# A two-block transformer kernel: the 16 extra tokens of the by-token projections computed feature-major and transposed, and v of the second block in 512-wide products

## The chip, the cores and the metric

The kernel runs on one core of a Trainium2 chip. The metric is device time in microseconds (us), the median of several executions. The engines are TensorE (PE, with its weight loads shown as a lane of its own, PEld), VectorE (DVE), ScalarE (ACT), GpSimd (POOL) and the queue that issues most transfers (SP).

## The reference

The input is x of 512 tokens by 1024 features; 16 learned extra tokens are put ahead of them, T = 528 tokens in all. What matters here:

```
# first block
xn   = rmsnorm(concat(meta_tokens, x), ln1_w)
proj = xn @ w_in            # dq, dk, dv, gq, gk, gv, gr, zf, zb
# dv (512 wide): values of a softmax attention over all 528 tokens, 4 heads
# gv (512 wide): values of a gated linear attention, 4 heads
h = x + concat(da, go) @ w_out
h = h + peer_ffn(rmsnorm(h, ln2_w))
x = rmsnorm(h, final_norm_w)
# second block
z = rmsnorm(x, mix_norm) @ w_in_2      # z_pool, u, v, two gates; 1024 features each
v = rmsnorm(gelu(v), sgu_norm)         # then mixed over the tokens of each chunk of 128
...                                    # gates, a convolutional feed-forward, a last gate
```

All of it is float32 in and out.

## The kernel before, in words

**Products.** Activations lie feature-major: X is [128 partitions, 8, 528], the feature index split over partitions and KD = 8 slices, the 512 tokens first and the 16 extra tokens (N_META) last. Every operand of a large product is split into a high and a low part in a rounded format, and `mm3` (line 97) adds three matmuls per slice: high by high, high by low, low by high. A matmul has a stationary operand, which a weight load brings into the array, and a moving operand, whose columns stream through. `load_w` fetches a weight tile and `split` makes its two parts, the high one by an ACT copy (line 73), the low one by a DVE subtraction (line 74), each in two halves, with four buffers of each kind. A weight tile of 512 KB therefore gives two high and two low halves of [128, 512 elements].

**Two layouts of a result.** Most projections keep features on the partitions: weights are stationary, tokens move (`product`, `halved`, `linear`). The values dv, gv and v are needed with tokens on the partitions, so there the tokens are stationary and weight columns move. For gv and dv that is `by_token` (lines 296 to 308). It handles 256 weight columns at a time, from two weight tiles of four slices: for each of five token blocks (four of 128, one of the 16 extra tokens) it takes a PSUM bank, runs 24 matmuls, and ACT scales the result by the token's norm factor `rcol` and writes it (line 307). After each token block it yields.

`by_token` is called four times: once directly for the first half of gv, then three times inside the generator `projections` (second half of gv, two halves of dv). `projections` is a list of filler work that other stages draw from: `fill(n)` advances it by n yields, and `until(...)` advances it until a named result exists. The linear attention draws 20 yields in its first half and 16 in its second; then the softmax attention draws one per query tile in heads 0 and 1, a few in heads 2 and 3 (at most four, since AFTER is 4), two after head 3, and the rest at its end. The last items of `projections` are eight output projections `out_proj(4, m)`, each 12 matmuls of 512 columns and one yield. The softmax attention itself goes, for each head and query tile, through `scores` (matmul line 646, maximum, exponential line 653), transposes (line 666) and `values` (line 676).

The order of instructions on each engine is made from the order of the program by a list scheduler that works with its own estimates of durations, so an instruction can be placed ahead of earlier ones of its engine that are not ready by those estimates.

**v of the second block.** `branches` computes v with tokens on the partitions: for each half f2 of the 1024 features it holds four PSUM banks of 512 columns, one for each token block, and fills each bank in two parts of 256 columns from weight tiles of four slices by 256 columns. Between the two parts of the first half `factors` computes the norm statistics, which end in a reduction by PE (line 110), a second one (line 1162), and the per-token factors (line 1327). The Gelu of line 1335 then reads the banks.

Of the kernel before, what the change touches and what calls it, by code (L numbers as in the profile page):

```python
# [8 lines left out]
F32 = mybir.dt.float32  # L9
# [6 lines left out]
ALU = mybir.AluOpType  # L16
# [4 lines left out]
P = 128  # L21
D = 1024
KD = D // P
SEQ = 512
NT = SEQ // P
N_META = 16
T = SEQ + N_META
# [162 lines left out]
def mixer_block(c):  # L190

    nc, tc, I = c.nc, c.tc, c.I
    with ExitStack() as ctx:
        bp = ctx.enter_context(tc.tile_pool(name="b1", bufs=1))
        wk = ctx.enter_context(tc.tile_pool(name="b1k", bufs=2))
# [3 lines left out]
        def bank(name="mm"):  # L199
            return ps.tile([P, 512], F32, tag="mm", name=name)  # L200
# [15 lines left out]
        xh, xl = operands(c, T)  # L216
# [32 lines left out]
        R = bp.tile([P, T], F32, name="rstd1")  # L249
# [13 lines left out]
        for t in range(NT + 1):  # L263
            n = P if t < NT else N_META
            if t % 2 == 0:
                g2 = two(2 * SEQ) if t < NT else bank()[:, None, :]
            o = g2[:, t % 2, :]
# [20 lines left out]
        rcol = bp.tile([P, NT + 1], F32, name="rcol")  # L288
        o = bank("pr")
        for t in range(NT + 1):  # L290
            n = P if t < NT else N_META
# [4 lines left out]
        def by_token(src, res, fs):  # L296

            for f in fs:
                fs = slice(256 * f, 256 * f + 256)
                ws = [src(False) for _ in range(2)]  # L300
                for t in range(NT + 1):
                    n = P if t < NT else N_META
                    tk = slice(t * P, t * P + n)
                    o = bank()[:n, :256]
                    c.mm3([o], [((xh[:, k, tk], xl[:, k, tk]), [(ws[k // 4][0].row(k % 4), ws[k // 4][1].row(k % 4))])
                                for k in range(KD)])
                    nc.scalar.mul(res[:n, t, fs], o, rcol[:n, t:t + 1])
                    yield

        gv = bp.tile([P, NT + 1, 512], F32, name="gv")  # L310
# [176 lines left out]
        for p in range(2):  # L487
# [65 lines left out]
            for l, s in enumerate(LEVELS + (0,)):  # L553
# [22 lines left out]
                for t in range(NT):  # L576
                    tk = slice(t * P, (t + 1) * P)
# [11 lines left out]
            for i, h in enumerate((2 * p, 2 * p + 1)):  # L589
                hs = slice(64 * i, 64 * i + 64)  # L590
                o = bank("go")
                for t in range(NT):
                    tk = slice(t * P, (t + 1) * P)
# [26 lines left out]
        o = bank()  # L620
# [509 lines left out]
def second_block(c):  # L1130
    nc, tc, I, X = c.nc, c.tc, c.I, c.X[:, :, :SEQ]
    with ExitStack() as ctx:
        bp = ctx.enter_context(tc.tile_pool(name="b2", bufs=1))
        wk = ctx.enter_context(tc.tile_pool(name="b2k", bufs=2))
# [13 lines left out]
        n1 = Norm(c, wk, c.fmw)  # L1148
        R = bp.tile([P, SEQ], F32, name="R01")
# [17 lines left out]
            nc.vector.tensor_tensor(R, R, R0, ALU.mult)  # L1167
            return R0, o

        jobs = [(I["w_v"][f, q], (4, 256)) for f in range(4) for q in range(2)]  # L1170
        jobs.insert(4, (I["w_zpool"][0], (KD, P)))
        for g in range(len(WINDOWS)):
            jobs += [(I[name][2 * g + k], (KD, P)) for name in ("w_zpool", "w_u") for k in range(2) if g or k or name == "w_u"]
# [8 lines left out]
        weights = c.weights(jobs)  # L1182
# [6 lines left out]
        with ExitStack() as actx:  # L1189
# [5 lines left out]
            for m in range(KD):  # L1195
                t = []
# [11 lines left out]
            for m in range(KD):  # L1208
                o = linear(of(mh, ml))
# [91 lines left out]
def branches(c, ap, wk, n1, R, factors, s_out, y_out, bank, tmp, weights, linear):  # L1301

    nc, tc, I, X = c.nc, c.tc, c.I, c.X[:, :, :SEQ]
    vn = ap.tile([P, NT, D], F32, tag="mh", name="vn")
    misc = ap.tile([P, 4, D], F32, tag="ml", name="misc")
    junk, gn, bs, ws = (misc[:, i, :] for i in range(4))
    bs, ws = (v.rearrange("p (h t) -> p h t", h=KD) for v in (bs, ws))
    sc = ap.tile([P, 3, NT], F32, name="sc")
    mk = ap.tile([P, P], F32, name="mk")
    inv = ap.tile([P, len(WINDOWS), PAD], F32, name="inv")  # L1310

    for f2 in range(2):
        banks = [bank() for _ in range(NT)]
        for f in range(2):
            for q in range(2):
                wh, wl = next(weights)
                for t in range(NT):
                    tk = slice(t * P, (t + 1) * P)
                    c.mm3([banks[t][:, f * 256:f * 256 + 256]],
                          [((n1.hi[:, 4 * q + k, tk], n1.lo[:, 4 * q + k, tk]), [(wh.row(k), wl.row(k))]) for k in range(4)],  # L1320
                          first=q == 0, last=q == 1)
            if f2 == 0 and f == 0:
                R0, o = factors()
        if f2 == 0:
            z0 = linear(n1.pairs)
            for t in range(NT):
                nc.tensor.matmul(o[:, t:t + 1], R[0:1, t * P:(t + 1) * P], c.ones[0:1, 0:1], start=True, stop=True)
            nc.vector.tensor_copy(sc[:, 0, :], o[:, :NT])
            nc.sync.dma_start(out=gn, in_=I["sgu_norm"].partition_broadcast(P))
            nc.sync.dma_start(out=bs, in_=I["b_spatial"].partition_broadcast(P))  # L1330
            nc.sync.dma_start(out=ws, in_=I["w_spatial"])
            nc.sync.dma_start(out=mk, in_=I["c_causal"])
            nc.sync.dma_start(out=inv, in_=I["c_inv"])
        for t in range(NT):
            nc.scalar.activation(out=vn[:, t, f2 * 512:(f2 + 1) * 512], in_=banks[t], func=AF.Gelu, scale=sc[:, 0, t:t + 1])
    nc.vector.tensor_tensor(ws, ws, mk[:, None, :].to_broadcast([P, KD, P]), ALU.mult)
    for t in range(NT):
        i = nc.scalar.activation(out=junk, in_=vn[:, t, :], func=AF.Square, accum_out=sc[:, 1, t:t + 1])
    with tc.issue_after(i.ins):
        nc.scalar.preload_act_table_set("natural_log_exp_and_others")  # L1340
    nc.scalar.activation(out=sc[:, 2, :], in_=sc[:, 1, :], func=AF.Ln, scale=1.0 / D, bias=c.eps)
    nc.scalar.activation(out=sc[:, 2, :], in_=sc[:, 2, :], func=AF.Exp, scale=-0.5)
    for t in range(NT):
        nc.vector.scalar_tensor_tensor(vn[:, t, :], vn[:, t, :], sc[:, 2, t:t + 1], gn, op0=ALU.mult, op1=ALU.mult)

    def pool(w, g, y, o):

        z = wk.tile([P, PAD + SEQ], F32, tag="z", name="z")
        nc.vector.memset(z[:, :PAD], 0.0)
        nc.vector.tensor_tensor(z[:, PAD:], o, R, ALU.mult)  # L1350
        s, d = z, 1
        while d < w:
            n = wk.tile([P, PAD + SEQ], F32, tag="zs", name="zs")
            nc.vector.memset(n[:, :PAD], 0.0)
            nc.vector.tensor_tensor(n[:, PAD:], s[:, PAD:], s[:, PAD - d:PAD + SEQ - d], ALU.add)
            s, d = n, 2 * d
        nc.vector.scalar_tensor_tensor(y, s[:, PAD:], 1.0 / w, z[:, PAD:], op0=ALU.mult, op1=ALU.subtract)
        nc.vector.tensor_tensor(y[:, :PAD], s[:, PAD:2 * PAD], inv[:, g, :], ALU.mult)
        nc.vector.tensor_tensor(y[:, :PAD], y[:, :PAD], z[:, PAD:2 * PAD], ALU.subtract)

    def gated(h):
        o = linear(n1.pairs)
        u = tmp("g0")
        nc.vector.tensor_tensor(u, o, R, ALU.mult)
        nc.scalar.activation(out=u, in_=u, func=AF.Gelu)
        o = bank()
        for t in range(NT):
            nc.tensor.matmul(o[:, t * P:(t + 1) * P], vn[:, t, h * P:(h + 1) * P], ws[:, h, :], start=True, stop=True)
        m = tmp("g1")
        nc.vector.tensor_tensor(m.rearrange("p (t i) -> p t i", t=NT), o.rearrange("p (t i) -> p t i", t=NT),  # L1370
                                bs[:, h:h + 1, :].to_broadcast([P, NT, P]), ALU.add)
        nc.vector.tensor_tensor(m, m, u, ALU.mult)
        split_plain(c, s_out[0][:, h, :], s_out[1][:, h, :], m)

    for g, w in enumerate(WINDOWS):
        ph = wk.tile([P, 2, SEQ], F32R, tag="ph", name="ph", bufs=1)
        pl = wk.tile([P, 2, SEQ], F32R, tag="pl", name="pl", bufs=1)
        for k in range(2):
            y = tmp("g0")
            pool(w, g, y, linear(n1.pairs) if g or k else z0)  # L1380
            split_plain(c, ph[:, k, :], pl[:, k, :], y)
        for h in (2 * g, 2 * g + 1):
            gated(h)
            nc.vector.scalar_tensor_tensor(X[:, h, :], X[:, h, :], c.final_norm_w[:, h:h + 1], R0, op0=ALU.mult, op1=ALU.mult)
        wh, wl = next(weights)
        for m in range(2):
            o = bank()
            c.mm3([o], [((wh.row(2 * m + k), wl.row(2 * m + k)), [(ph[:, k, :], pl[:, k, :])]) for k in range(2)])
            f = 2 * g + m
            split_scaled(c, y_out[0][:, f, :], y_out[1][:, f, :], o, c.pool_scale_2[:, f:f + 1])  # L1390
# [13 lines left out]
def pack_t(w):  # L1404
    k, m = w.shape
    return np.ascontiguousarray(w.reshape(k // P, P, m // P, P).transpose(2, 1, 0, 3))


def pack_n(w, kc=4, m=256):
    k, n = w.shape  # L1410
    return np.ascontiguousarray(w.reshape(k // (kc * P), kc, P, n // m, m).transpose(3, 0, 2, 1, 4))
# [6 lines left out]
def pack(a):  # L1418
# [23 lines left out]
    I["u_t"] = np.ascontiguousarray(u.reshape(P, NKEYS, KD, P).transpose(1, 3, 2, 0))  # L1442
    I["v_t"] = np.ascontiguousarray(v.reshape(P, NKEYS, 2, 512).transpose(1, 0, 2, 3))
    w = a["w_in_2"][0]
    I["w_zpool"], I["w_u"], I["w_v"] = pack_t(w[:, :D]), pack_t(w[:, D:2 * D]), pack_n(w[:, 2 * D:3 * D])
    I["w_gates"] = np.stack([pack_t(w[:, 3 * D:4 * D]), pack_t(w[:, 4 * D:])])
    I["w_branch"] = np.stack([pack_t(a["w_branch_a_2"][0]), pack_t(a["w_branch_b_2"][0])])
    I["w_out2"] = pack_t(a["w_out_2"][0])
# [56 lines left out]
```

## Time and profile before

| | |
|---|---|
| median of 3 executions | 2463.1 us |
| lowest, highest | 2460.37, 2471.28 us |
| the profiled execution, its own time | 2468.12 us |
| its span, first to last instruction | 2466.4 us |
| mean granted TensorE clock in it | 0.987 of full speed |

The profile and the trace are of one execution; its span and its own time are 1.7 us apart. A busy share counts time with at least one instruction of the engine in flight. Matmuls overlap: one lasts longer than the step from its start to the next one's start. The granted clock is 1.0 at 2.4 GHz and 0.5 at 1.2 GHz.

### The profile page before, as it was taken

What the parts mean: (1) busy time and instruction counts of PE and PEld (TensorE: products, weight loads), DVE (VectorE), ACT (ScalarE), POOL (GpSimd) and SP (SyncE); (2) the same over time, 40 slices, a digit from 0 to 9 for tenths busy, and PEclk for the clock granted to TensorE, in tenths of its full rate; (3) what the DMA queues carried; (4) which work ended last, traced back from release to release, by engine and by line L of the source; (5) the groups of instructions that cost most, each with busy time, mean ns of one, the idle gap of its engine ahead of it and who ended that gap; (6) DMA issues with size and microseconds to landing.
All of it is one profiled execution on the core that took longest, in us unless ns stands there. A gap on an engine that the chain in (4) does not pass through costs nothing.

```text
span 2466.4 us, 34671 instructions
## 1 busy us (share of the span) xinstructions
PE 2402.0 (97%) x12603; PEld 2084.6 (85%) x12603; DVE 1758.2 (71%) x3426; ACT 1194.7 (48%) x2155; POOL 367.3 (15%) x260
## 2 busy tenths in 40 slices
PE   8999899999999999999999998999999999999998
PEld 7887578999999999888778788878888888888888
DVE  5775659999899886886676775866764456777436
ACT  5434553446788995433333333335433335544335
POOL 0000000001333323333242342420000000000000
PEclk9999999999999999999999999999999999999999
DMA  4210033356999999988888889953232232233332
GB/s 138 69 52 26 27 128 137 104 187 202 335 358 348 329 332 361 364 299 295 309 283 289 321 291 311 311 175 106 87 98 94 95 102 96 94 97 98 94 105 103
DMA packets 170297, 471.81 MB, mean 191 GB/s; under 512 B 14060, under 2 KB 66157, under 8 KB 166798
## 3 DMA queue, kind: packets, MB, share of 16 engines
q1 hardware_dynamic: 133262, 335.37, 39.8%
q0 software_dynamic: 36864, 134.23, 15.7%
q8 instruction: 99, 1.62, 0.3%
q14 instruction: 72, 0.59, 0.1%
HBM read 421.31 MB, written 48.23 MB: 190 GB/s over the span
## 4 chain that ended last, share of the span: by engine, by line
PE 62%; DMA 9%; issue 6%; DVE 5%; POOL 2%; ACT 1%; SPq 0%; DVEq 0%; POOLq 0%; ACTq 0%
PE mm L97 49%; PE acc L1105 8%; DMA at<-Ad 3%; DMA row<-in_v_t_dram,ev 3%; PE G L987 3%; POOL row L802 2%; DVE wlo L74 1%; DMA row<-in_peer_u_dram,eu 1%; DMA wraw<-in_v_t_dram 1%; DVE acc L823 1%; PE sc L886 1%; DMA gt<-Gd 1%; DVE row L815 0%; SPq L1064 0%; DVE eq L939 0%
## 5 line engine op out<-in xcount | busy, mean ns | idle before, releaser
L73 ACT CAST whi<-wraw 128x512 fp32r<-128x512 f32 (+3 forms) x902 | 547.4, 609 | 900.8 <-PE mm L97 521.3
L74 DVE TENSOR_TENSOR wlo<-wraw,whi 128x512 fp32r<-128x512 f32 (+3 forms) x902 | 595.4, 670 | 260.6 <-ACT whi L73 256.6
L97 PE MATMUL mm<-hi,whi 128*128 128x384 f32 (+3 forms) x2016 | 721.4, 363 | 16.3 <-ACT fresh L790 9.3
L97 PE MATMUL mm<-lo,whi 128*128 128x384 f32 (+3 forms) x2016 | 717.9, 361 | 0.7 <-DVE lo L182 0.5
L97 PE MATMUL mm<-hi,wlo 128*128 128x384 f32 (+3 forms) x2016 | 717.0, 361 | 0.4 <-DVE wlo L74 0.4
L97 PEld LDWEIGHTS mm<-hi,whi 128*128 128x128 f32 (+1 forms) x2016 | 376.3, 188 | 56.2 <-ACT fresh L790 10.2
L97 PEld LDWEIGHTS mm<-hi,wlo 128*128 128x128 f32 (+1 forms) x2016 | 376.0, 188 | 38.2 <-DVE wlo L74 1.7
L97 PEld LDWEIGHTS mm<-lo,whi 128*128 128x128 f32 (+1 forms) x2016 | 376.1, 188 | 38.1 <-issue 1.7
L1105 PE MATMUL acc<-wlo,wh 128*128 128x512 f32 x768 | 304.0, 396 | 20.9 <-DVE wlo L74 20.7
L802 POOL DMA_INDIRECT row<-in_peer_u_dram,eu x128 | 168.4, 1316 | 930.0 <-DMA wraw<-in_u_t_dram 544.4
L1105 PE MATMUL acc<-whi,wl 128*128 128x512 f32 x768 | 302.2, 394 | 0.0
L802 POOL DMA_INDIRECT row<-in_v_t_dram,ev x128 | 198.7, 1552 | 333.6 <-ACT whi L73 239.2
L1105 PE MATMUL acc<-whi,wh 128*128 128x512 f32 x768 | 248.1, 394 | 0.0
L823 DVE SCALAR_TENSOR_TENSOR acc<-row,act,acc 128x1024 f32<-128x1024 f32 x128 | 163.8, 1280 | 46.0 <-DMA row<-in_v_t_dram,ev 46.0
L1105 PEld LDWEIGHTS acc<-wlo,wh 128*128 128x128 f32 x768 | 146.3, 191 | 56.1 <-DVE wlo L74 25.7
L815 DVE SCALAR_TENSOR_TENSOR row<-row,hn 128x1024 f32<-128x1024 f32 x128 | 155.6, 1218 | 26.6 <-DMA row<-in_peer_u_dram,eu 26.3
L1105 PEld LDWEIGHTS acc<-whi,wh 128*128 128x128 f32 x768 | 146.0, 190 | 30.7
L1105 PEld LDWEIGHTS acc<-whi,wl 128*128 128x128 f32 x768 | 146.3, 190 | 30.3
L984 ACT ACTIVATE oa<-oa,tr 128x128 f32<-128x128 f32 x384 | 122.6, 393 | 21.5 <-DVE oa L982 21.1
L987 PE MATMUL G<-ob,oa 128*128 128x128 f32 x768 | 113.1, 277 | 1.2 <-ACT oa L984 1.2
L987 PEld LDWEIGHTS G<-ob,oa 128*128 128x128 f32 x768 | 108.9, 191 | 2.3 <-ACT oa L984 2.2
L988 ACT COPY gst<-G 128x512 f32<-128x512 f32 x96 | 102.1, 1070 | 16.1 <-PE G L987 15.2
(359 smaller groups left out, 3048.6 us busy)
## 6 DMA issues: line engine op xcount, KB each, us to landing
wraw<-in_u_t_dram SPq DMA_DIRECT2D x128, 512.0 KB, 5.3
wraw<-in_v_t_dram SPq DMA_DIRECT2D x128, 512.0 KB, 7.1
Gd<-gst SPq DMA_DIRECT2D x24, 1024.0 KB, 6.3
gt<-Gd SPq DMA_DIRECT2D x16, 1536.0 KB, 13.0
wraw<-in_w_up_dram SPq DMA_DIRECT2D x44, 512.0 KB, 3.4
Ad<-ast SPq DMA_DIRECT2D x24, 768.0 KB, 5.6
at<-Ad SPq DMA_DIRECT2D x24, 768.0 KB, 12.3
wraw<-in_w_pq_dram SPq DMA_DIRECT2D x16, 512.0 KB, 4.2
```

What stands on the lines that cost most here:

```text
L73: self.step = nc.scalar.copy(hi[i], x)
L74: nc.vector.tensor_tensor(lo[i], x, hi[i].bitcast(F32), ALU.subtract)
L97: nc.tensor.matmul(o, a, b, start=first and ps == 0 and i == 0, stop=last and ps == 2 and i == n - 1)
L802: i = nc.gpsimd.indirect_dma_start(out=t, out_offset=None, in_=table, in_offset=bass.IndirectOffsetOnAxis(ap=idx[:, s:s + 1], axis=0))
L815: nc.vector.scalar_tensor_tensor(u, u, 1.0, hn, op0=ALU.mult, op1=ALU.mult, accum_out=c.act3[:, s:s + 1])
L823: nc.vector.scalar_tensor_tensor(c.acc3, v, c.act3[:, s:s + 1], c.acc3, op0=ALU.mult, op1=ALU.add)
L886: nc.tensor.matmul(o[:, t * P:(t + 1) * P], q[:, t * P:(t + 1) * P], keys[:, f, :], start=True, stop=True)
L984: nc.scalar.mul(oa[:, i, :], oa[:, i, :], tr[:, 2, b0 + i:b0 + i + 1])
L987: nc.tensor.matmul(o[:, i * P:(i + 1) * P], oa[:, i, :], ob[:, i, :], start=True, stop=True)
L988: nc.scalar.copy(st[:, :, b0 - t0:b0 - t0 + TB].rearrange("p j n -> p n j"), o.rearrange("p (n j) -> p n j", n=TB))
L1105: nc.tensor.matmul(acc[2 * t + hf], x[:, jb, tk], y.row(hf), start=n_done == 1 and pi == 0, stop=last2 and bi == len(batch) - 1 and pi == 2)
```

## The change

In `by_token` the 16 extra tokens leave the loop over token blocks. They are computed first, feature-major: for each of the two groups of 128 weight columns, the weights are stationary and the 16 tokens move, into one bank of 32 columns. DVE multiplies this by the norm factors R of those tokens into the tile `me`. After the second token block, PE transposes the two parts of `me` into a bank and ACT copies it to its place. The loop yields four times instead of five.

In `branches`, v's weight tiles become two slices by 512 columns instead of four slices by 256; a tile now fills all 512 columns of the four banks, and four tiles make a half. `factors` stands behind the third of the four tiles.

```diff
             for f in fs:
                 fs = slice(256 * f, 256 * f + 256)
                 ws = [src(False) for _ in range(2)]
-                for t in range(NT + 1):
-                    n = P if t < NT else N_META
-                    tk = slice(t * P, t * P + n)
-                    o = bank()[:n, :256]
+
+                mt = slice(SEQ, T)
+                o = bank()[:, :2 * N_META]
+                for i in range(2):
+                    c.mm3([o[:, i * N_META:(i + 1) * N_META]],
+                          [((ws[k // 4][0].row(k % 4)[:, i * P:(i + 1) * P], ws[k // 4][1].row(k % 4)[:, i * P:(i + 1) * P]),
+                            [(xh[:, k, mt], xl[:, k, mt])]) for k in range(KD)])
+                me = wk.tile([P, 2, N_META], F32, tag="kmt", name="me")
+                nc.vector.tensor_tensor(me, o.rearrange("p (i n) -> p i n", i=2), R[:, None, SEQ:].to_broadcast([P, 2, N_META]), ALU.mult)
+                for t in range(NT):
+                    tk = slice(t * P, (t + 1) * P)
+                    o = bank()[:, :256]
                     c.mm3([o], [((xh[:, k, tk], xl[:, k, tk]), [(ws[k // 4][0].row(k % 4), ws[k // 4][1].row(k % 4))])
                                 for k in range(KD)])
-                    nc.scalar.mul(res[:n, t, fs], o, rcol[:n, t:t + 1])
+                    nc.scalar.mul(res[:, t, fs], o, rcol[:, t:t + 1])
+                    if t == 1:
+                        o = bank()[:N_META, :256]
+                        for i in range(2):
+                            nc.tensor.transpose(o[:, i * P:(i + 1) * P], me[:, i, :], c.ident)
+                        nc.scalar.copy(res[:N_META, NT, fs], o)
                     yield
...
-        jobs = [(I["w_v"][f, q], (4, 256)) for f in range(4) for q in range(2)]
+        jobs = [(I["w_v"][f, q], (2, 512)) for f in range(2) for q in range(4)]
...
     for f2 in range(2):
         banks = [bank() for _ in range(NT)]
-        for f in range(2):
-            for q in range(2):
-                wh, wl = next(weights)
-                for t in range(NT):
-                    tk = slice(t * P, (t + 1) * P)
-                    c.mm3([banks[t][:, f * 256:f * 256 + 256]],
-                          [((n1.hi[:, 4 * q + k, tk], n1.lo[:, 4 * q + k, tk]), [(wh.row(k), wl.row(k))]) for k in range(4)],
-                          first=q == 0, last=q == 1)
-            if f2 == 0 and f == 0:
+        for q in range(4):
+            wh, wl = next(weights)
+            for t in range(NT):
+                tk = slice(t * P, (t + 1) * P)
+                c.mm3([banks[t]],
+                      [((n1.hi[:, 2 * q + k, tk], n1.lo[:, 2 * q + k, tk]), [(wh.row(k), wl.row(k))]) for k in range(2)],
+                      first=q == 0, last=q == 3)
+            if f2 == 0 and q == 2:
                 R0, o = factors()
```

## Rows read from the trace of the kernel before

**Rows 1.** The page: busy shares, and the chain that ended last by engine.

```profile
PE 2402.0 (97%) x12603; PEld 2084.6 (85%) x12603; DVE 1758.2 (71%) x3426; ACT 1194.7 (48%) x2155; POOL 367.3 (15%) x260
...
PE 62%; DMA 9%; issue 6%; DVE 5%; POOL 2%; ACT 1%; SPq 0%; DVEq 0%; POOLq 0%; ACTq 0%
```

**Rows 2.** Windows: length, busy by engine, granted clock, DMA; by_token calls, v stage.

```profile
33.05:51.40 18.35, 18.35 (x127) 15.63 (x126) 3.11 (x7) 8.98 (x19) 0.00 (x0) 0.91 0.01 4
70.50:88.00 17.50, 17.50 (x167) 16.36 (x166) 10.51 (x26) 5.75 (x9) 0.00 (x0) 1.00 0.10 31
177.20:194.00 16.80, 16.80 (x154) 15.62 (x152) 12.76 (x26) 7.10 (x13) 0.00 (x0) 1.00 0.01 1
214.00:240.80 26.80, 25.61 (x173) 19.64 (x171) 15.63 (x36) 12.31 (x31) 0.00 (x0) 1.00 0.01 1
1676.20:1739.70 63.50, 63.50 (x456) 59.55 (x455) 38.24 (x62) 35.30 (x59) 0.00 (x0) 1.00 0.25 82
```

**Rows 3.** Timeline of PE (start, duration in us): a 16-token block, its successor.

```profile
85.20 0.29 PE L97 MATMUL mm<-whi,hi 128*16 128x256 f32 x1
...
87.95 0.40 PE L97 MATMUL mm<-hi,whi 128*128 128x512 f32 x1
```

**Rows 4.** Weight loads grouped by shape: busy us, mean ns, idle before.

```profile
L97 PEld LDWEIGHTS mm<-whi,lo 128*128 128x128 f32 x256 | 49.4, 194 | 0.0
...
L97 PEld LDWEIGHTS mm<-wlo,hi 128*16 128x16 f32 x32 | 3.0, 94 | 0.9 <-issue 0.3
```

**Rows 5.** Timeline of PE: short matmuls with loads of 128 columns.

```profile
52.83 0.39 PE L327 MATMUL mm<-tri,g 16*128 16x16 f32 x2
53.15 0.38 PE L322 MATMUL mm<-tri,g 128*128 128x128 f32 x1
...
1709.58 1.05 PE L1327 MATMUL ps_r<-ones,R 1*128 1x1 f32 x8
```

**Rows 6.** Timeline of PE in the last head of the softmax attention.

```profile
308.46 0.81 PE L646 MATMUL mm<-k,q 64*128 64x264 f32 x1 [2.11 <-ACT pe L653]
...
318.36 0.60 PE L666 MATMUL mm<-ident,pe 128*128 128x128 f32 x4
```

**Rows 7.** Instructions of the tile km: minimum, median, maximum ns.

```profile
L281 DVE TENSOR_TENSOR km<-mm,rstd x2: 152/154/155, 24.8 to 64.4; 128x16 f32<-128x16 f32 x2
```

**Rows 8.** Timeline of PE in the v stage.

```profile
1693.47 1.02 PE L110 MATMUL ps_r<-nacc,ones 128*128 128x512 f32 x2
...
1710.56 0.39 PE L97 MATMUL mm<-whi,hi 128*128 128x256 f32 x1
...
1728.78 0.40 PE L97 MATMUL mm<-hi,whi 128*128 128x512 f32 x1
...
1739.69 0.38 PE L1368 MATMUL mm<-misc,vn 128*128 128x128 f32 x2
```

**Rows 9.** Windows: stretches around falls of the granted clock (column after POOL).

```profile
31.00:34.40 3.40, 3.40 (x23) 2.61 (x24) 0.91 (x3) 0.93 (x2) 0.00 (x0) 1.00 0.53 154
34.40:37.80 3.40, 3.40 (x14) 2.64 (x13) 0.00 (x0) 0.00 (x0) 0.00 (x0) 0.50 0.00 0
37.80:41.20 3.40, 3.40 (x26) 2.89 (x25) 0.00 (x0) 2.78 (x6) 0.00 (x0) 1.00 0.00 0
...
256.20:263.10 6.90, 6.76 (x22) 3.40 (x20) 5.62 (x13) 2.21 (x6) 0.00 (x0) 0.51 0.00 0
...
266.50:269.90 3.40, 3.40 (x5) 1.33 (x4) 2.28 (x7) 0.79 (x2) 0.00 (x0) 0.50 0.00 0
...
307.40:314.30 6.90, 5.84 (x16) 4.29 (x17) 4.71 (x14) 3.21 (x9) 0.00 (x0) 0.51 0.14 40
```

**Rows 10.** Timeline of PE ahead of the first fall.

```profile
31.43 0.59 PE L268 MATMUL mm<-w,zT 33*128 33x512 f32 x1
31.95 1.18 PE L292 MATMUL pr<-ones,rstd 1*128 1x1 f32 x10
```

**Rows 11.** Waits of PE from 230 to 331 us: total us, times, longest.

```profile
PE mm L646 <- ACT pe L653: 8.2, 5, 2.6
```

More of the change, by code (lines that the diff above doesn't have):

```diff
@@ L1444, in pack @@
     w = a["w_in_2"][0]
-    I["w_zpool"], I["w_u"], I["w_v"] = pack_t(w[:, :D]), pack_t(w[:, D:2 * D]), pack_n(w[:, 2 * D:3 * D])
+    I["w_zpool"], I["w_u"], I["w_v"] = pack_t(w[:, :D]), pack_t(w[:, D:2 * D]), pack_n(w[:, 2 * D:3 * D], 2, 512)
     I["w_gates"] = np.stack([pack_t(w[:, 3 * D:4 * D]), pack_t(w[:, 4 * D:])])
```

## The prediction

> **What bounds the kernel now.** I read the page's busy shares and its chain first [rows 1]. TensorE (PE) has a matmul in flight for 97% of the span, and the chain that ended last runs through PE for 62% of it, more than through any other resource. The first question for an edit that touches matmuls is therefore whether PE is full where the edit lies. The windows answer it [rows 2]: in the stretches that hold the four calls of by_token, PE is busy for 18.35 of 18.35, 17.50 of 17.50, 16.80 of 16.80 and 25.61 of 26.80 us, and through the v stage for 63.50 of 63.50. So PE time removed or added there goes to the end nearly one to one, while ScalarE (ACT) and VectorE (DVE) have room. A busy PE hides how fast it goes, since matmuls overlap. What counts is the step from one start to the next, read from the timeline, and the granted clock, read from windows.
>
> **The change part by part: what is removed.** Each call of by_token ends with 24 matmuls whose stationary operand is the 16 tokens and whose moving operand is 256 weight columns. One such block starts at 85.20 and the next matmul behind it at 87.95 [rows 3]: 2.75 us, a step of 0.115. Four calls give 11.0 us. An ACT eviction of a 16-partition tile goes too.
>
> **What is added.** Operands swap: 128 weight columns become stationary and 16 tokens move. That takes 2 x 8 x 3 = 48 matmuls per call, each with its own load of 128 columns. The trace has no such matmul of 128 rows. Its stream of columns is short, so the load decides. A load of 16 columns lasts 94 ns and one of 128 lasts 194 [rows 4]: 100 ns for 112 columns, so about 0.114 us for 128 if each column costs the same. The nearest matmuls agree: eight with a 128-column load and one moving column take 1.05 us in all [rows 5], from which the last one's own time comes off (0.25, an estimate: the 256-column ones beside it last 0.28): 0.80 over seven steps, 0.114. I take 0.115. Below it I set 0.107, a little under both; above it 0.133, from two matmuls of 16 columns with a 128-column load, though of 16 rows: 0.39 us in all, or 0.13 without the last one's own 0.26 (the same estimate), and 0.16 each from 52.83 to the next start at 53.15 [rows 5]. So a call pays 48 x 0.115 = 5.5 us where it paid 2.75.
>
> Two transposes per call come on top. Four of them in a row take 0.60 us [rows 6], so about 0.11 a step, 0.2 us per call. The scaling by R is a DVE operation on 128x32; its neighbour on 128x16 takes 154 ns [rows 7]. The transposes stand behind two whole token blocks, 48 matmuls or 5.8 us after the narrow ones, so DVE has that long before PE waits; without that cover it would cost up to about 1 us per call, the wait for one operation ahead of it in DVE's queue. The new copy by ACT replaces the eviction that went. I count all three at nothing.
>
> By_token alone: 5.5 + 0.2 - 2.75 = +2.95 us per call, **+11.8 us** for four. With 0.107 it is +10.3, with 0.133 it is +15.3.
>
> **The v stage.** 384 matmuls of 256 columns become 192 of 512. From 1710.56 to 1728.78 there are 151 of the narrow kind: 0.1207 a step. From 1728.78 to 1739.69 there are 48 wide ones: 0.2273 [rows 8]. Two narrow less one wide is 0.0141 us, times 192 is **-2.7 us**. Loads (eight of 512 KB) and splits (128x512) keep their sizes. The statistics (factors) now stand behind three of four weight tiles of the first half instead of two. In the trace their first reduction on PE is at 1693.47 [rows 8], about where three tiles end when the stage starts near 1673: 72 x 0.227 = 16.4 plus the slow start. I count the move at nothing. If it is late instead, the Gelu evictions and then the four banks of the second half are, and it costs up to 3 us.
>
> Sum so far: 11.8 - 2.7 = **+9.1 us**.
>
> **The clock.** This is the larger unknown. The windows show the granted clock at half, 1.2 instead of 2.4 GHz, after stretches in which PE did little streaming, and being busy did not save it [rows 9]: from 31.0 to 34.4 PE is busy for all 3.40 us, but until about 33.1 with matmuls of 33 rows or 1 row [rows 10], and from 34.4 to 37.8 the clock is 0.50. Then 14 matmuls start where 26 start in the next equal stretch. The other falls in this block come in the attention, where matmuls have 64 rows and gaps. A new narrow block streams 16 columns in each 0.115 us, a sixteenth of what the block before it streams, for 5.5 us on end. I expect that to look like the first case. Its price from rows: the four low stretches of this block last 3.4, 6.9, 3.4 and 6.9 us, 5.2 on average [rows 9]; at half clock half of that is lost, 2.6 us. Four blocks: **+10.4 us**. The ends are 0 (the clock holds, because the loads count as work) and about 5 us per block, 20 in all, if the narrow block itself runs at 0.23 a step for most of its length and the wide matmuls behind it start low.
>
> **Moved work.** by_token hands control back after each token block, and now does so four times instead of five. Three of its calls feed the fillers of the linear attention and the softmax attention, so everything behind them comes three fillers earlier: three of the four output projections that so far run in the last head's tail move up to the second head. The tail is where PE waits for softmax (8.2 us in five waits over the attention [rows 11], one of 2.11 before 308.46 [rows 6]). A block of output projection is 12 matmuls of about 0.23, 2.8 us, so up to 8.4 us could be uncovered there; against it, the idle time and the low clock in the second head (3.4 us lost of the 6.9 from 256.2) could be filled. Nothing at the middle, 5 us to either side.
>
> One rule of the Trainium skill speaks against the swap itself: TensorEngine Tiling (Array Packing), section When to Use Tiling, says that where the moving dimension is 64 or less one should exchange stationary and streaming operands. The 16 tokens are the stationary operand today; the change does the opposite. The loads of 94 and 194 ns say the same in this kernel, and the sum above is what it costs.
>
> **The rivals.**
> - *Load-bound and the clock falls* (the forecast): 9.1 + 10.4 = +19.5 us. For it: [rows 4, 5, 9]. Against it: no row shows 128-row loads with almost no streaming.
> - *Load-bound, the clock holds*: +9.1 us, 2472 on the median. It needs the loads to count for the clock.
> - *Narrow matmuls are cheap*, the other side: the load hides wholly and only moving columns pace PE. Then 16 columns cost a sixteenth of 0.115, 48 of them 0.35 us, and a call gains 2.75 - 0.35 - 0.2 = 2.2; with the v stage that is -8.8 - 2.7 = -11.5 us, 2452. It decides as soon as a step is below 0.053 (2.55 us over 48). Against it stands the 0.114 of one-column matmuls, though those have one row. The Trainium skill gives this rule: TensorE: Matmul & The Clock Gate, section Back-to-back issue gap, puts matmuls of 1 to 64 columns at an issue floor of about 25 ns. By it a call would pay 1.2 us and the whole would be an estimated -8 us. No row here shows steps that short with a 128-column load.
> - *The shifted fillers decide*: the tail of the attention is uncovered by 8.4 us on top of +9.1: +17.5, 2481, with the clock unchanged in the projections.
>
> **How the numbers follow.** The profiled execution took 2468.1 us, 5.0 above the median of 2463.1, inside the runs' spread of 2460.4 to 2471.3. On it the forecast is 2487.6; carried to the median it is **2482**. About 0.5%, 12.3 us, is what a measurement of this kernel tells from no change. Chances: forecast 0.57, clock holds 0.30, cheap narrow matmuls 0.08, fillers 0.05. The first is slower by over 0.5% in about 0.85 of its cases, the second in 0.25, the third never (faster in 0.2 of its own), the fourth in 0.8: slower 0.60, faster 0.03 (a lucky filler order under the second included), same 0.37. The range runs from the clock-holds case with luck in the attention, 2472 - 6 = 2466, to the forecast with the dear clock, 2463 + 9 + 20 = 2492, plus 2 for a step above 0.115: 2494. The cheap case lies below it.
>
> **What would show it.** In the profile after: 192 matmuls 128*128 128x16 at line 97, at a step near 0.115 or, at half clock, near 0.23; windows over the four narrow blocks with a granted clock well below 1 within or just behind them; the v stage at 0.227 a step and 2.7 us shorter; pairs of transposes with no wait of PE for DVE before them; less PE work between the last scores and the last values of the attention. The prediction is wrong if the narrow step is far below 0.1, if the clock stays at 1.00 through the blocks, or if the attention changes by more than 5 us.

## The result, and the profile after

The changed kernel takes 2488.3 us (median of 6, 2481.1 to 2491.0) beside 2461.7 for the kernel before on the same chips (median of 6, 2455.2 to 2471.3): a ratio of 1.0097, 95% interval 1.0074 to 1.0120, or 18 to 30 us more. It is slower, as forecast; 2482 was predicted, 2466 to 2494 the range. The profiled execution took 2491.0 us, its span is 2489.3, and its mean granted clock 0.981 of full speed.

The page of the kernel after: busy shares, the granted clock in tenths over 40 slices, and the chain that ended last.

```profile
PE 2422.0 (97%) x12515; PEld 2102.7 (84%) x12515; DVE 1757.5 (71%) x3430; ACT 1193.1 (48%) x2155; POOL 381.2 (15%) x260
...
PEclk8998999999999999999999999999999999999999
...
PE 67%; DMA 8%; issue 4%; DVE 3%; POOL 1%; ACT 1%; SPq 0%; DVEq 0%; POOLq 0%; ACTq 0%
```

Beside [rows 1] PE has 88 instructions fewer and is busy 20 us longer; the other engines hardly change. Two of the first four slices of the clock show an 8. The windows of the kernel after say when (columns as in [rows 2], the granted clock behind POOL). In each group the rows with 0.50 are whole low stretches, the others their surroundings.

```profile
29.50:32.90 3.40, 3.40 (x14) 1.24 (x12) 1.59 (x3) 1.86 (x3) 0.00 (x0) 1.00 0.56 181
32.90:53.40 20.50, 20.50 (x81) 17.21 (x82) 1.86 (x6) 5.98 (x12) 0.00 (x0) 0.50 0.02 5
53.40:61.98 8.58, 8.58 (x75) 8.54 (x75) 2.37 (x4) 3.62 (x8) 0.00 (x0) 1.00 0.00 1
...
80.70:84.10 3.40, 3.40 (x37) 3.23 (x33) 3.21 (x9) 1.53 (x2) 0.00 (x0) 1.00 0.51 159
84.10:94.30 10.20, 10.20 (x50) 10.20 (x50) 0.36 (x2) 0.00 (x1) 0.00 (x0) 0.50 0.00 0
...
196.70:203.50 6.80, 6.80 (x34) 6.80 (x34) 2.14 (x5) 0.02 (x1) 0.00 (x0) 0.50 0.00 0
...
237.70:244.50 6.80, 6.80 (x34) 6.80 (x34) 0.19 (x1) 0.00 (x0) 0.00 (x0) 0.50 0.00 0
...
292.30:295.70 3.40, 3.40 (x11) 2.73 (x9) 1.29 (x7) 2.50 (x7) 0.00 (x0) 0.50 0.05 18
...
340.10:346.90 6.80, 6.40 (x19) 4.87 (x20) 4.38 (x14) 3.34 (x11) 0.00 (x0) 0.50 0.11 38
```

There is one low stretch at each of the four narrow blocks: 20.5, 10.2, 6.8 and 6.8 us, 44.4 in all before rounding, where the kernel before had one of 3.4 in the same calls [rows 9]. The trace is of one execution; the others are like it, for the mean granted clock is 0.981 to 0.984 in the six of the changed kernel, and 0.986 to 0.990 in the eighteen of the kernel before that were run beside e1 to e4. PE is busy for every microsecond of all four. From 84.10 on, its 10.20 us of busy time hold 50 matmuls; the 3.40 us ahead of it held 37.

The timeline of PE in the kernel after shows the steps: first call, second call, v stage.

```profile
33.27 0.38 PE L97 MATMUL mm<-hi,whi 128*128 128x16 f32 x1
...
45.63 0.56 PE L97 MATMUL mm<-whi,hi 128*128 128x256 f32 x1
...
81.30 0.26 PE L97 MATMUL mm<-lo,whi 128*128 128x16 f32 x1
...
83.98 0.26 PE L97 MATMUL mm<-lo,whi 128*128 128x16 f32 x1
84.09 0.36 PE L97 MATMUL mm<-hi,wlo 128*128 128x16 f32 x1
84.31 0.36 PE L97 MATMUL mm<-hi,whi 128*128 128x16 f32 x1
...
1697.52 0.47 PE L97 MATMUL mm<-whi,hi 128*128 128x512 f32 x1 [2.55 <-DVE X L1134]
...
1762.06 0.38 PE L1380 MATMUL mm<-misc,vn 128*128 128x128 f32 x2
```

From 81.30 to 83.98 lie 24 steps of 0.112 us; then, with the clock at half, a step is 0.21 to 0.22. The step thus slows with the clock; that its load sets it is for e4 to show. The v stage runs from 1697.52 to 1762.06, 64.5 us; in the kernel before it ran from the matmul below to the one at 1739.69 [rows 8], 66.8:

```profile
1672.88 0.55 PE L97 MATMUL mm<-whi,hi 128*128 128x256 f32 x1 [2.55 <-DVE X L1121]
```

So 2.3 us are gained there.

The cheap parts: the groups of the tile me in the kernel after (minimum, median, maximum ns, first and last start), the transposes on PE and the scaling on DVE.

```profile
L319 PE MATMUL mm<-ident,me x8: 270/272/273, 56.1 to 248.0; 128*16 128x128 f32 x8
L309 DVE TENSOR_TENSOR me<-mm,rstd x4: 190/191/192, 45.8 to 240.4; 128x32 f32<-128x32 f32 x4
```

The first scaling starts at 45.8 and the first transpose at 56.1, ten microseconds later: DVE had its time, and the costliest groups show no idle time of PE ahead of the transposes.

```profile
L97 PE MATMUL mm<-hi,whi 128*128 128x16 f32 x64 | 20.3, 317 | 0.0
...
L319 PE MATMUL mm<-ident,me 128*16 128x128 f32 x8 | 1.5, 271 | 0.0
```

The waits of PE from 250 to 360 us in the kernel after (in total, times, longest) stand for the attention.

```profile
PE mm L659 <- ACT pe L666: 5.1, 4, 3.8
PE mm L679 <- DVE pe L672: 3.7, 4, 1.4
PE da L689 <- ACT aT L680: 3.3, 4, 1.6
PE ps_r L110 <- ACT sq L693: 1.3, 1, 1.3
```

The wait of [rows 11], 8.2 us in five, is 5.1 in four, but three others stand beside it: 13.4 us in this stretch, against 8.8 in the stretch of [rows 11]. Whether that is the moved fillers or the later arrival of everything is a question for e5 and e6.

**Where the time is lost.** The scores with the keys are the first matmuls behind the first block. The tile sc in the kernel before and then in the kernel after (minimum, median, maximum ns, first and last start):

```profile
L886 PE MATMUL sc<-keys,q x128: 270/275/378, 380.3 to 474.4; 128*128 128x128 f32 x128
```

```profile
L899 PE MATMUL sc<-keys,q x128: 270/275/377, 405.4 to 499.5; 128*128 128x128 f32 x128
```

They begin at 405.4, and at 380.3 before: 25.1 us later. The v stage starts 24.6 later, and the end of the span is 22.9 later. So the whole loss is there before these scores begin, and the v stage gives 2.3 back. In the table below their first matmul is the mark, since the long peer stage behind it moves by some 10 us from one trace to the next even where nothing in it was changed.

### The profile page after: what moved, and what is told of

The parts are those of the page before. It is cut to its first block, busy times and chain, and to the rows that moved or that the text cites. A ratio compares the mean times of both kernels' runs of the same rounds, so it can differ in the third digit from the quotient of the medians.

```text
span 2489.3 us, 34498 instructions
## 1 busy us (share of the span) xinstructions
PE 2422.0 (97%) x12515; PEld 2102.7 (84%) x12515; DVE 1757.5 (71%) x3430; ACT 1193.1 (48%) x2155; POOL 381.2 (15%) x260
## 4 chain that ended last, share of the span: by engine, by line
PE 67%; DMA 8%; issue 4%; DVE 3%; POOL 1%; ACT 1%; SPq 0%; DVEq 0%; POOLq 0%; ACTq 0%
PE mm L97 51%; PE acc L1118 12%; PE G L1000 3%; DMA at<-Ad 3%; DMA row<-in_v_t_dram,ev 2%; POOL row L815 1%; DMA gt<-Gd 1%; DMA row<-in_peer_u_dram,eu 1%; DVE wlo L74 1%; DMA wraw<-in_v_t_dram 1%; PE sc L899 1%; DVE acc L836 1%; PE mm L1380 0%; SPq L1077 0%; DMA wraw<-in_w_ple_gate_dram 0%
## 5 line engine op out<-in xcount | busy, mean ns | idle before, releaser
L97 PE MATMUL mm<-hi,whi 128*128 128x384 f32 (+3 forms) x2080 | 744.5, 363 | 20.9 <-ACT fresh L803 14.3
L97 PE MATMUL mm<-hi,wlo 128*128 128x384 f32 (+3 forms) x2080 | 738.5, 360 | 1.7 <-DVE wlo L74 1.7
L97 PE MATMUL mm<-lo,whi 128*128 128x384 f32 (+3 forms) x2080 | 738.0, 359 | 0.3 <-DVE lo L182 0.2
L97 PEld LDWEIGHTS mm<-hi,whi 128*128 128x128 f32 (+1 forms) x2080 | 394.6, 191 | 61.3 <-ACT fresh L803 15.3
L97 PEld LDWEIGHTS mm<-lo,whi 128*128 128x128 f32 (+1 forms) x2080 | 394.6, 191 | 38.7 <-issue 3.2
L97 PEld LDWEIGHTS mm<-hi,wlo 128*128 128x128 f32 (+1 forms) x2080 | 394.6, 191 | 38.5 <-DVE wlo L74 3.0
L1118 PE MATMUL acc<-wlo,wh 128*128 128x512 f32 x768 | 301.8, 393 | 13.4 <-DVE wlo L74 13.4
L815 POOL DMA_INDIRECT row<-in_v_t_dram,ev x128 | 216.6, 1692 | 316.3 <-ACT whi L73 227.8
L1118 PEld LDWEIGHTS acc<-whi,wh 128*128 128x128 f32 x768 | 144.3, 188 | 30.1
L1001 ACT COPY gst<-G 128x512 f32<-128x512 f32 x96 | 102.1, 1070 | 14.5 <-PE G L1000 13.7
## 6 DMA issues: line engine op xcount, KB each, us to landing
gt<-Gd SPq DMA_DIRECT2D x16, 1536.0 KB, 12.1
at<-Ad SPq DMA_DIRECT2D x24, 768.0 KB, 12.1
```

Of the source, the lines that this page charges most:

```text
L97: nc.tensor.matmul(o, a, b, start=first and ps == 0 and i == 0, stop=last and ps == 2 and i == n - 1)
L815: i = nc.gpsimd.indirect_dma_start(out=t, out_offset=None, in_=table, in_offset=bass.IndirectOffsetOnAxis(ap=idx[:, s:s + 1], axis=0))
L1001: nc.scalar.copy(st[:, :, b0 - t0:b0 - t0 + TB].rearrange("p j n -> p n j"), o.rearrange("p (n j) -> p n j", n=TB))
L1118: nc.tensor.matmul(acc[2 * t + hf], x[:, jb, tk], y.row(hf), start=n_done == 1 and pi == 0, stop=last2 and bi == len(batch) - 1 and pi == 2)
```

## The experiments

The theory: the swapped blocks cost what their weight loads cost, and their thin streams bring the clock down. Rivals: the order of the fillers costs the time; the clock falls for a reason that isn't the narrow stream; the narrow step isn't set by the load.

**e1, e2: the halves of the change alone.** e1 has by_token as before and only this:

```diff
-        jobs = [(I["w_v"][f, q], (4, 256)) for f in range(4) for q in range(2)]
+        jobs = [(I["w_v"][f, q], (2, 512)) for f in range(2) for q in range(4)]
...
-                    c.mm3([banks[t][:, f * 256:f * 256 + 256]],
+                c.mm3([banks[t]],
```

e2 has the v stage as before and the changed by_token.

> Only v of the second block is 512 wide; by_token is as before. Both theories (clock and loads alone) expect the v stage, from its first matmul to the first one that mixes v, to go from 66.8 to about 64.5 us (2.3 us less, as in the changed kernel), and the whole to be 2 to 3 us faster, about 0.1%, which the times can hardly tell from no change.

> Only by_token is changed; v is as before. If the two parts do not act on each other, it is slower than before by what the whole change costs plus the 2.3 us that the v stage gave: 25 to 29 us, about 1.1%, with the same low stretches of the clock.

e1: 2462.4 beside 2462.8 us, ratio 0.9991 (0.9975 to 1.0007). The timeline of PE in e1 gives the v stage:

```profile
1672.64 0.47 PE L97 MATMUL mm<-whi,hi 128*128 128x512 f32 x1 [2.56 <-DVE X L1121]
...
1737.17 0.38 PE L1367 MATMUL mm<-misc,vn 128*128 128x128 f32 x2
```

64.5 us for 66.8: the 2.3 us show in the trace and are too small for the time. The traces of e1 and of the kernel before both have a low stretch of 3.4 us in this stage. Where a trace has none, the stage takes 65.4 us as it was (e2) and 62.9 when 512 wide (e7, below): 2.5 us less. e2: 2492.9, ratio 1.0104 (1.0080 to 1.0128), 20 to 32 us more, as expected. The whole loss belongs to by_token.

**e3: the narrow matmuls mixed into the stream.** The 48 no longer stand in one block: two follow every three wide ones in the first three token blocks, and the transposes stand behind the fourth.

```diff
+                        for ps_, (x, y) in enumerate(((xh, wh), (xh, wl), (xl, wh))):
+                            nc.tensor.matmul(o, x[:, k, tk], y, start=k == 0 and ps_ == 0, stop=k == KD - 1 and ps_ == 2)
+                            if ps_ and narrow:
+                                d, x2, y2, st_, sp_ = narrow.pop(0)
+                                nc.tensor.matmul(d, x2, y2, start=st_, stop=sp_)
```

> The changed kernel with the same 48 narrow matmuls and 48 loads per call, but two of them put behind every three wide ones of the first three token blocks instead of 48 in a row; the transposes stand after the fourth block. Theory clock: the loads cost what they did (0.112 us each, 2.7 us per call more than before), but the granted clock stays at 1.0 through the projections, so the whole is about 9 us slower than before, 16 to 20 faster than the change. Theory loads alone (the low clock is a companion that costs nothing of its own): as slow as the change, about 25 us.

2478.2 us, ratio 1.0063 (1.0040 to 1.0086). This expectation was missed: less than the change costs, but not the load alone. The windows of e3, first call and then the stretches of the later ones, say why:

```profile
29.60:33.00 3.40, 3.40 (x10) 1.03 (x11) 1.69 (x3) 2.23 (x4) 0.00 (x0) 1.00 0.51 170
33.00:67.10 34.10, 34.10 (x145) 30.62 (x145) 3.81 (x9) 8.33 (x16) 0.00 (x0) 0.50 0.02 8
67.10:85.00 17.90, 17.90 (x128) 16.62 (x128) 14.54 (x37) 11.74 (x22) 0.00 (x0) 1.00 0.25 89
...
180.00:200.00 20.00, 19.95 (x140) 15.65 (x139) 18.35 (x39) 6.29 (x9) 0.00 (x0) 1.00 0.17 53
215.00:245.00 30.00, 30.00 (x215) 25.26 (x213) 13.95 (x29) 10.36 (x22) 0.00 (x0) 1.00 0.11 36
```

In the third and fourth call the clock is full throughout, and in the second it stays full until the mixed part is over and then is low for 3.4 us. But in the first call the clock falls at 33.0, after the short matmuls that [rows 10] show ahead of the first fall, and stays at half for 34.1 us: the mixed stream doesn't raise a low clock as it keeps a full one. Four matmuls of 33 rows, 4 us in all, stand in that stretch too and in no later call, so the mixed stream isn't all that differs.

**e4, e7: more moving columns.** The load and the count of matmuls stay as in the changed kernel; 128 (e4) or 256 (e7) tokens move instead of 16. They compute the tokens ahead of the last 16 once more, and those results aren't used.

```diff
-                mt = slice(SEQ, T)
-                o = bank()[:, :2 * N_META]
+                mt = slice(T - P, T)
+                o = bank()[:, :2 * P]
```

> The changed kernel with 128 tokens as the moving operand of the narrow matmuls instead of 16; only the last 16 columns of each result are used, so it does eight times the streaming in the same 48 matmuls and loads per call. If the load sets the step, the step stays at 0.11 to 0.12 us; if columns add to it, it grows by 112 columns or 0.047 us to 0.16. Theory clock: streaming for about half of the time keeps the clock up, so doing more work makes it faster than the change: 9 us slower than before (12 to 18 if the columns add). Theory loads alone: at least as slow as the change, 25 us or more.

> As the run with 128 moving columns, with 256 tokens moving, of which the last 16 are used: sixteen times the streaming of the change, step 0.12 us as for the wide matmuls. Theory clock: the granted clock falls in no by_token call but the first, where it is low for 3.4 to 7 us as before; by the loads alone 48 x 0.12 + 0.2 - 2.75 = 3.2 us per call, 12.9 in all, less 2.3 of v: about 10 us slower than before, at most as slow as 128 columns (11 us). Theory loads alone: 25 us or more.

e4: 2474.2 us, ratio 1.0038 (1.0016 to 1.0061). e7: 2468.9, ratio 1.0017 (0.9991 to 1.0042). Eight and sixteen times the stream take less time than the changed kernel, as the theory of the clock expected and the loads alone did not. The timeline of PE in e4, one whole narrow block and the matmul behind it:

```profile
79.06 0.33 PE L97 MATMUL mm<-hi,whi 128*128 128x128 f32 x1
...
84.47 0.33 PE L97 MATMUL mm<-whi,hi 128*128 128x256 f32 x1
```

48 steps in 5.41 us, 0.113 each, the step of the 16-column ones at full clock: the moving columns don't enter it. That the load does is borne out by one pair in the kernel before: of the ten one-column matmuls at 31.95 [rows 10], the eight with a load of 128 columns have steps of 0.11 to 0.13, the last two, with a load of 16 columns, start 0.04 us apart. In e7, with 256 moving columns, the step is 0.120. The windows of e4, then of e7:

```profile
31.10:48.20 17.10, 17.10 (x71) 14.93 (x71) 2.39 (x6) 3.48 (x7) 0.00 (x0) 0.50 0.08 28
48.20:85.00 36.80, 36.80 (x292) 33.73 (x291) 21.50 (x52) 19.54 (x36) 0.00 (x0) 1.00 0.18 58
85.00:110.00 25.00, 25.00 (x196) 22.08 (x195) 16.28 (x33) 8.62 (x15) 0.00 (x0) 1.00 0.19 64
180.00:200.00 20.00, 20.00 (x161) 17.74 (x160) 14.59 (x30) 5.95 (x9) 0.00 (x0) 1.00 0.08 27
215.00:245.00 30.00, 29.60 (x203) 24.79 (x204) 12.05 (x29) 10.20 (x22) 0.00 (x0) 1.00 0.03 10
```

```profile
31.90:38.70 6.80, 6.80 (x32) 6.34 (x31) 0.91 (x3) 0.23 (x1) 0.00 (x0) 0.50 0.17 61
38.70:250.00 211.30, 210.87 (x1538) 181.69 (x1538) 130.81 (x269) 88.63 (x155) 0.00 (x0) 1.00 0.15 48
```

In both, the first low stretch is all the low time up to 250 us, so the three later calls run at full clock, where the changed kernel falls three times. What differs is the width of the stream alone. In the first call the fall isn't the narrow block's: in the changed kernel the clock is low from 32.90 and the block begins at 33.27. Its length varies with the same block: with 16 columns it is 20.5 us in the changed kernel, 23.9 in e2 and 13.7 in e5. So 17.1 with 128 columns is no shorter than those; only 6.8 with 256 stands apart, and that is one trace.

**e5: the yields.** One more behind the narrow block, so that the fillers get as many turns as before.

```diff
                 nc.vector.tensor_tensor(me, o.rearrange("p (i n) -> p i n", i=2), R[:, None, SEQ:].to_broadcast([P, 2, N_META]), ALU.mult)
+                yield
```

> The changed kernel with one more yield per call, behind the narrow block, so that the fillers are dealt out five to a call as before. If the order of fillers is a part of the loss, several us come back; if the narrow blocks and the clock are all of it, it stays 22 to 30 us slower than before. I expect the latter, within 4 us of the change at the start of the peer stage (25 us behind before).

2488.0 us, ratio 1.0089 (1.0060 to 1.0119): the loss of the change, with the fillers' turns given back, as expected.

**e6: everything but the swap.** The 16 tokens come first and there are four yields, as in the changed kernel, but the tokens stay stationary and 256 columns move, with no transposes; v is 512 wide.

```diff
-                for t in range(NT + 1):
+                for t in (NT, *range(NT)):
...
-                    yield
+                    if t < NT:
+                        yield
```

> All of the change but the swap of operands: the 16 tokens come first and the loop yields four times, but they stay stationary with 256 columns moving, without transposes; v is 512 wide. Theory clock and loads: as fast as v alone, 2.3 us faster than before plus or minus 4 us for the fillers. If the fillers or the order within by_token cost something, it is slower than before by that.

2464.4 us, ratio 0.9992 (0.9967 to 1.0017): no difference from the kernel before. The first matmuls of the tile sc with the keys (minimum, median, maximum ns, first and last start), in e6 and then in e5, show the two sides:

```profile
L888 PE MATMUL sc<-keys,q x128: 270/275/377, 380.6 to 474.7; 128*128 128x128 f32 x128
```

```profile
L900 PE MATMUL sc<-keys,q x128: 270/275/378, 402.0 to 496.1; 128*128 128x128 f32 x128
```

380.6 is what it was before (380.3); 402.0 is 21.7 us later. The swap is the loss, not the moves around it. The two also answer the question of the waits. From the first score matmul to the last value matmul PE is idle for 9.4 us before and 12.1 after; in e5, late but with its turns, it is 10.2, and in e6, on time but without them, 12.6. So the longer waits come from the moved fillers.

## Why the prediction was right

The table makes the sum for each kernel from its own trace, up to the first matmul of sc with the keys. "Own" is 4 x (48 steps + 0.2 - 2.75). "Clock" is half of the low time beyond that of the kernel before (3.4 us up to 250 us, 17.1 in the attention behind it). The last column is the interval of the ratio times the median of the kernel before.

| | low time to 250 us | own | clock to 250 us | clock in attention | sum | measured there | whole, 95% |
|---|---|---|---|---|---|---|---|
| after | 44.4 | +11.3 | +20.5 | -3.4 | +28.4 | +25.1 | +18 to +30 |
| e2, tokens only | 44.4 | +11.3 | +20.5 | -1.7 | +30.1 | +28.7 | +20 to +32 |
| e5, five yields | 34.1 | +11.3 | +15.4 | -1.7 | +25.0 | +21.7 | +15 to +29 |
| e3, mixed | 37.5 | +11.3 | +17.1 | -1.7 | +26.7 | +21.3 | +10 to +21 |
| e4, 128 columns | 17.1 | +11.4 | +6.9 | -3.4 | +14.9 | +12.2 | +4 to +15 |
| e7, 256 columns | 6.8 | +12.8 | +1.7 | -3.4 | +11.1 | +9.7 | -2 to +10 |
| e6, no swap | 13.7 | 0 | +5.1 | -3.4 | +1.7 | +0.3 | -8 to +4 |
| e1, v only | 6.8 | 0 | +1.7 | -1.7 | 0 | +0.4 | -6 to +2 |

In e6, 10.2 of the 13.7 us lie at 241, where its attention has begun. In every row the shift measured at the mark, less 2.3 us where v is 512 wide, lies inside the interval of the whole.

- **The narrow blocks, +11.8 predicted: right.** 0.112 a step at full clock for 0.115; four calls pay 11.3 us. e4 shows that the columns don't set it: eight times as many, the same step. So the rival of cheap narrow matmuls falls. The figure beside it, about 25 ns (the Trainium skill, TensorE: Matmul & The Clock Gate, section Back-to-back issue gap), isn't what a matmul with a load of its own takes here: 112 ns were measured. That section gives it for the isolated gap and says itself that in a stream of loads and matmuls both set the spacing, which the prediction left out. The section LDWEIGHTS of the same page of the Trainium skill takes the columns divided by 1.2 for a load in ns, an estimated 107 ns for 128; that is near the full-clock step, while at half clock the step was 213.
- **Transposes, scaling, copy, factors at nothing or 0.2 us a call: right.** No idle time of PE stands ahead of the transposes, and the v stage shows no late statistics: PE is busy in it for 61.20 of 61.20 us from 1700.9.
- **The v stage, -2.7 predicted: -2.3 measured,** in the changed kernel and in e1 alike, and -2.5 at full clock throughout (e7 beside e2).
- **The clock, +10.4 predicted: right mechanism, wrong size.** The term was mis-sized. It took four stretches of 5.2 us, the mean of low stretches whose cause was a few short matmuls or gaps. Measured were 20.5, 10.2, 6.8 and 6.8 us, with 3.4 there before: (44.4 - 3.4) / 2 = +20.5 us, the "dear" end of the prediction's bound. Half is a little too much: from 0.213 a step to 0.112 (16 columns) or 0.118 (256 columns, the median step in the changed kernel) the low time loses 0.47 or 0.45 of itself, so an estimated +18.5. What the term underrated is that a fall lengthens its own cause: at half clock a narrow block takes up to 48 x 0.213 = 10.2 us instead of 5.4. In the first call the clock is at half from the block's start, and with two matmuls of 33 rows among its own (2.0 us) it runs from 33.27 to 45.63; behind it the wide matmuls, with two more of 33 rows among them (2.0 us), run low for another 7.8 us. The fall itself isn't the narrow block's there: it came 0.37 us ahead of the block, so the block lengthened a low stretch that the kernel before has too. That the narrow stream is the cause of the later three falls, and not the place or the count of matmuls, is shown by e4 and e7, where only the width differs and those falls are gone. With 128 columns the three later calls are what the rival "clock holds" describes; with 16 they aren't.
- **Fillers and attention, 0 within 5 us: inside its bound.** The sum of the table is 3.3 us too high in the first row, and 1.4 to 5.4 in e2 to e7. Adding the steps of PE's timeline, from start to start up to the mark, shows where. The matmuls at the four calls (those of 16 tokens or 16 columns, the transposes, and their neighbours of 256 columns, 33 rows and 1 row) come to 28.7 us more than before, where own and clock made 31.8. All else comes to 3.6 less, which is nearly the -3.4 of the low time: the score matmuls 6.2 less, PE's idle time 3.2 more, the rest 0.6 less. So the difference lies in the calls: 2 us are the half that is too much, and 0.7 are the removed blocks, whose steps add up to 11.7 us and not 11.0; 0.6 stays open. The moved fillers nearly cancel in themselves: the scores and the idle time are -0.8 and -0.8 in e5, which gives the turns back, and -3.3 and +4.1 in e6, which doesn't. Nor did the tail get worse: from the last score matmul to the last value matmul it was 16.4 us and is 11.1, with 20 matmuls of 512 columns in it for 43.

On the profiled executions 2491.0 stands against a forecast of 2487.6, 3.4 us more: the narrow blocks and the clock +6.5 (28.7 for 22.2), the attention -3.6, the v stage +0.4, in all +3.3. So a part of that closeness is luck: the clock's term was about 8 us too small, and an attention that came out 3.6 us cheaper, which wasn't forecast, hid some of it. On the medians 2482 was 6 us low; most of the other 3 is that the profiled execution stood 5.0 us above its median before and 2.7 after.

The rule that the prediction cites against the swap (the Trainium skill, TensorEngine Tiling (Array Packing), section When to Use Tiling) names the exchange of operands together with tiling the array by columns, which no kernel here does. For the exchange alone the pair of e6 and the changed kernel, which differ in the swap and its transposes, agrees with it: 0.9992 and 1.0097 of the kernel before, 2464.4 and 2488.3 us. No version here beats the kernel before by more than its measurement tells; e1, e6 and, within its interval, e7 equal it.

## What to carry to other kernels

Cost a matmul with a load of its own by the longer of load and stream: with 128 stationary columns, 16 moving ones cost what 128 do (0.112 and 0.113 us a step), so a narrow operand belongs on the stationary side. Then ask what its stream does to the clock: a PE that is busy without a gap can still fall to half speed, as at 84.10 in the kernel after, and the loss goes on in the wide matmuls behind. Price such a fall by the time that the block takes at half clock and what follows it, not by the length of falls seen elsewhere.

## What the runs showed of the hardware that was not expected

- With a load of 128 columns the step is 0.112 us for 16 moving columns, 0.113 for 128 and 0.120 for 256 at full clock. At half clock 16, 128 and 256 columns all take 0.213 to 0.214.
- What a stream does to the clock depends on the clock that it meets: in e3 the mixed stream ran its third and fourth call at 1.00 where it met a full clock, and 34.1 us at 0.50 where it met a low one, there with four matmuls of 33 rows among it, PE being busy for at least 19.95 of 20 us in each.
- Behind the first narrow block of the changed kernel, matmuls of 256 columns, with two of 33 rows among them, ran from 45.63 to 53.40 at half clock before it rose, 7.8 us; in the kernel before the whole fall in this call lasted 3.4 [rows 9].
